# mLSTM heads: from token-major to feature-major by block transposes on VectorE and a DRAM scratch

## The chip, the cores and the metric

The kernel runs on one core of one Trainium2 chip. The metric is the time of one execution in device microseconds (us). In the profile PE is TensorE (PEld its weight loads), DVE is VectorE, ACT is ScalarE, POOL is GpSimd and SP is SyncE, which issues the weight loads from DRAM. Each engine works through its own queue in order. A DMA is issued from an engine's queue, is carried out by the 16 DMA engines, and signals when it has landed.

## What is computed

The reference is a two-layer model on 512 tokens of width 1024: a dilated attention layer, a feed-forward layer, an mLSTM layer and a second feed-forward layer, each with a residual. The change lies in the mLSTM layer. Cut to what matters:

```python
def mlstm_mixer(xn, w_in, conv_w, conv_b, ig_bias, fg_bias, head_gain, w_out):
    proj = xn @ w_in
    ...
    h = mlstm_chunkwise(q, k, vh, ig, lf)          # 8 heads, 512 tokens, 128 values each
    h = h * lax.rsqrt(jnp.mean(h * h, axis=-1, keepdims=True) + RMS_EPS)
    h = h.reshape(B, S, D_MODEL) * head_gain
    return (h * jax.nn.sigmoid(o_pre)) @ w_out
```

For each head a 512 x 128 block of numerators is divided by a denominator for each token, normalized over its 128 values, multiplied by a gate, and all eight heads together go through the output matrix.

## The kernel before

Activations are kept feature-major: a tile has 128 features on the partitions and the 512 tokens along them. Matrix products are made in two parts for precision: each operand is split into a high and a low part, and three matmuls of 128x512 (high-high, high-low, low-high) are added up in PSUM. Weights come in chunks of 512 KB by a DMA on SP into `wraw`; ACT writes the high part (L208) and DVE the low part (L209). In the profile `mqk`, `mv`, `mo` and `mwo` are the products for queries and keys, for values, for the output gate, and with the output matrix; `mwo_k_l` is the low part of a weight chunk of the last of these. `f1j` is the first product of the feed-forward layer that follows.

The mLSTM scan is computed in its quadratic form over 512 tokens, one head after the other, in four steps that are spread over the projections as work to put between them:

- `decay` makes the exponents: a matmul `m0nb` (for head 0) into the PSUM bank of tag `t`, DVE adds the mask (`m0d`), ACT the exponentials (`m0e`).
- `scores` multiplies queries and keys (`m0s`; `ks`, `qs` and `ql` are their split parts, made by `stack`), and DVE multiplies the products into `m0e`.
- `numerators` multiplies by the values (`m0num`, 10 matmuls, which the profile shows as 20 records) into two PSUM banks of tag `o`, of which there are two in all. DVE takes the denominators (`m0rr`), ACT sums the squares (`m0j` into `m0s` of 4 columns), DVE makes an inverse square root by Newton's steps (`m0rq`, small operations on 128x4, each dependent on the last), and four DVE operations scale the numerators into `m0yt` (L1365). This tile is token-major: 128 tokens of a block on the partitions, and four blocks of 128 features next to each other.
- `outputs` turns it: four PE transposes of 128x128 into a bank of tag `t` (`m0yT`, L305), and one ACT copy into `y` (L1374), which is feature-major.

`HEAD_AT` gives for each head the ticks at which the four steps are put into the program; a tick passes with each chunk of a projection. The framework that builds the queues then orders the instructions of each engine by what it expects to be ready, so that small pieces of one step stand between matmuls of a projection, and a change in one place also moves instructions elsewhere.

During `mo` the gate is multiplied in: DVE scales (`og`, L1397), ACT takes a tanh (L1398), DVE multiplies it into `y` (L1399). At the end `y` is split by ACT into `yo_h` (L226) and by DVE into `yo_l` (L227), and `mwo` reads these. `mwo` goes through pairs of 128 output features; each pair takes the heads 0 to 3 and then 4 to 7. Its results are added to the residual `hn` by DVE (L790).

Elsewhere the kernel has the path that the change uses here. In the attention layer `turn` puts values through a DVE transpose of 32x32 blocks (`a3vB`, L673), four DMAs on POOL for each into DRAM (`a3vD`, L675) and one read back (`a3v`, L677); the last layer does the same with the residual (`hB` L1427, `hD` L1430, `ht` L1437).

Of the kernel before, what the change touches and what calls it, by code (L numbers as in the profile page):

```python
# [11 lines left out]
F32 = mybir.dt.float32  # L12
F32R = mybir.dt.float32r
I32 = mybir.dt.int32
AF = mybir.ActivationFunctionType
ALU = mybir.AluOpType
AX = mybir.AxisListType
P = 128

SEQ = 512  # L20
D = 1024
KC = D // P
TB = SEQ // P
# [11 lines left out]
RUN_AT = (2, 3, 5, 10)  # L35
LAST_AT = (2, 4)
STACK_AT = (9, 11, 15, 17)
HEAD_AT = ((9, 10, 12, 14), (10, 11, 13, 15), (12, 13, 15, 17), (13, 14, 16, 18), (15, 16, 18, 19), (16, 17, 19, 21),
           (18, 19, 21, 22), (19, 20, 21, 23))
W_BUFS = 3  # L40
SPLITS = [(0, 0), (0, 1), (1, 0)]

# [28 lines left out]
def tile_hybrid_dilated_attn_mlstm(  # L71
# [4 lines left out]
    nc = tc.nc  # L76
# [3 lines left out]
    def pool(stack, name, **kw):  # L80
        return stack.enter_context(tc.tile_pool(name=name, bufs=1, **kw))
# [4 lines left out]
    ps = pool(ctx, "psum", space=bass.MemoryType.PSUM)  # L86
# [96 lines left out]
    def rsqrt_newton(tp_pool, v, n, name, y=None):  # L183

        if y is None:
            y = tp_pool.tile([P, n], F32, tag="rs_y%d" % n, name=name + "_y", bufs=2)
        a = tp_pool.tile([P, n], F32, tag="rs_a%d" % n, name=name + "_a", bufs=2)
        nc.vector.tensor_single_scalar(a.bitcast(I32), v.bitcast(I32), 1, op=ALU.arith_shift_right)
        nc.vector.tensor_scalar(y.bitcast(I32), a.bitcast(I32), -1, 0x5F3759DF, op0=ALU.mult, op1=ALU.add)
        for _ in range(3):  # L190
            nc.vector.scalar_tensor_tensor(a, y, -0.5, y, op0=ALU.mult, op1=ALU.mult)
            nc.vector.tensor_tensor(a, a, v, op=ALU.mult)
            nc.vector.scalar_tensor_tensor(y, a, 1.5, y, op0=ALU.add, op1=ALU.mult)
        return y
# [8 lines left out]
    def split_chunk(chunk):  # L203

        raw, n, view, name = chunk
        hi = wp.tile([P, 1024], F32R, tag="whi", name=name + "_h", bufs=W_BUFS)
        lo = wp.tile([P, 1024], F32R, tag="wlo", name=name + "_l", bufs=W_BUFS)
        nc.scalar.activation(hi[:, :n], raw[:, :n], AF.Copy)  # L208
        nc.vector.tensor_tensor(lo[:, :n], raw[:, :n], hi[:, :n].bitcast(F32), op=ALU.subtract)  # L209
        return view(hi), view(lo)  # L210
# [4 lines left out]
    def weight_chunk(w2d, ch, c0, n, name):  # L215

        src = w2d[ch * 4 * P:(ch * 4 + n) * P, c0:c0 + 256].rearrange("(k p) n -> p k n", p=P)
        return load_chunk(src, [P, n, 256], name)
# [85 lines left out]
    def transpose_into(dst_ps, i, src, n=P):  # L304
        nc.tensor.transpose(dst_ps[:, i * n:(i + 1) * n], src, ident)  # L305
# [36 lines left out]
    npl = pool(ctx, "norm")  # L342
    h = [hp.tile([P, SEQ], F32, tag="h", name="h%d" % k, bufs=KC + 1) for k in range(KC)]

    with ExitStack() as actx:
# [3 lines left out]
        R = 32  # L349
# [758 lines left out]
    with ExitStack() as fctx:  # L1108
        fp = pool(fctx, "ffn0")
        a, ready = ffn_in(0, fp, pair, rbc, hook,  # L1110
                          lambda ch: split_chunk(weight_chunk(ffn_w_out[0], ch, 0, 4, "fo0_k%d" % ch)))
# [16 lines left out]
    w_in2 = mlstm_w_in[0]  # L1128
    with ExitStack() as mctx:
        mp = pool(mctx, "mlstm")  # L1130
        H = HEADS
        blk = lambda t: t.rearrange("p (b s) -> p b s", b=TB)
        FB = 32 * (TB - 1) + H

        def y_tile(k, name):
            return mp.tile([P, SEQ], F32, tag="my%d" % k, name=name)
# [23 lines left out]

        vaug = mp.tile([P, TB, H, P + 1], F32, name="vaug")
        for tb in range(TB):
# [11 lines left out]

        graw = mp.tile([P, KC, 2 * H], F32, name="graw")
        nc.scalar.dma_start(graw, w_in2[:, 3 * D:3 * D + 2 * H].rearrange("(k p) n -> p k n", p=P))
        bias2 = mp.tile([H, 2], F32, name="gbias")
        nc.scalar.dma_start(bias2[:, 0:1], mlstm_ig_bias.rearrange("o h -> h o"))
        nc.scalar.dma_start(bias2[:, 1:2], mlstm_fg_bias.rearrange("o h -> h o"))

        sel = mp.tile([P, H, P], F32R, name="sel")
        nc.gpsimd.memset(sel.bitcast(F32), 0.0)
# [83 lines left out]
        i = 0  # L1266
# [23 lines left out]
        def stack(p):  # L1290

            for i in range(2):
                own, oth = slice(i * 64, i * 64 + 64), slice(64 - i * 64, 128 - i * 64)
                q, k = qk[p][own], qk[4 + p][own]
                ks = mp.tile([P, SEQ], F32R, tag="ks%d" % i, name="ks%d_%d" % (p, i), bufs=2)
                qs = mp.tile([P, SEQ], F32R, tag="qs%d" % i, name="qs%d_%d" % (p, i), bufs=2)
                nc.scalar.activation(ks[own], k, AF.Copy)  # L1297
                nc.vector.tensor_tensor(ks[oth], k, ks[own].bitcast(F32), op=ALU.subtract)
                nc.scalar.activation(qs[own], q, AF.Copy)
                nc.scalar.activation(qs[oth], q, AF.Copy)  # L1300
                ql = mp.tile([P, SEQ], F32R, tag="ql%d" % i, name="ql%d_%d" % (p, i), bufs=2)
                nc.vector.tensor_tensor(ql[own], q, qs[own].bitcast(F32), op=ALU.subtract)
                nc.gpsimd.tensor_copy(ql[oth], ql[own].bitcast(F32))
                stacks[2 * p + i] = (ks, qs, ql)

        y = [None] * H
        decays, sms, yts = {}, {}, {}

        def decay(hh):
            nm = "m%d" % hh  # L1310
# [25 lines left out]
        def numerators(hh):  # L1336
            nm = "m%d" % hh
            sm = sms[hh]
            num = [ps.tile([P, 512], F32, tag="o", name=nm + "num", bufs=2) for _ in range(2)]
            nv = lambda qb: num[qb // 2][:, (qb % 2) * 256:(qb % 2) * 256 + P + 1]  # L1340
            for qb in range(TB):
                for kb in range(qb + 1):
                    o = (qb - kb) * P
                    nc.tensor.matmul(nv(qb), sm[kb][:, o:o + P], vaug[:, kb, hh, :],
                                     start=(kb == 0), stop=(kb == qb))

            rr = mp.tile([P, TB], F32, tag="rr", name=nm + "rr", bufs=2)
            aa = mp.tile([P, TB], F32, tag="aa", name=nm + "aa", bufs=2)
            s2 = mp.tile([P, TB], F32, tag="s2", name=nm + "s2", bufs=2)
            for t in range(2):  # L1350
                den = num[t].rearrange("p (a b) -> p a b", a=2)[:, :, P]
                nc.vector.tensor_copy(rr[:, 2 * t:2 * t + 2], den)
            nc.vector.scalar_tensor_tensor(aa, rr, -1.0, rr, op0=ALU.mult, op1=ALU.max)
            nc.vector.tensor_tensor(aa, aa, bcol[:, npair:, hh], op=ALU.max)
            nc.vector.reciprocal(rr, aa)
            for qb in range(TB):
                junk = mp.tile([P, P], F32, tag="junk", name=nm + "j", bufs=2)
                nc.scalar.activation(junk, nv(qb)[:, :P], AF.Square, scale=rr[:, qb:qb + 1],
                                     accum_out=s2[:, qb:qb + 1])
            nc.vector.tensor_scalar(s2, s2, 1.0 / P, EPS, op0=ALU.mult, op1=ALU.add)  # L1360
            rq = rsqrt_newton(mp, s2, TB, nm + "rq")
            nc.vector.tensor_tensor(rr, rr, rq, op=ALU.mult)
            yt = mp.tile([P, SEQ], F32, tag="yt", name=nm + "yt", bufs=2)
            for qb in range(TB):
                nc.vector.tensor_scalar(yt[:, qb * P:(qb + 1) * P], nv(qb)[:, :P], rr[:, qb:qb + 1], None,  # L1365
                                        op0=ALU.mult)
            yts[hh] = yt

        def outputs(hh):
            tp = ps.tile([P, 512], F32, tag="t", name="m%dyT" % hh, bufs=1)  # L1370
            for qb in range(TB):
                transpose_into(tp, qb, yts[hh][:, qb * P:(qb + 1) * P])
            y[hh] = y_tile(hh, "y%d" % hh)
            nc.scalar.activation(y[hh], tp, AF.Copy)  # L1374

        def at_tick(t, fn):
            defer(base + t - tick[0], fn)
        at_tick(8, exponents)
        for p, t in enumerate(STACK_AT):
            at_tick(t, lambda p=p: stack(p))  # L1380
        for hh, ts in enumerate(HEAD_AT):
            for t, fn in zip(ts, (decay, scores, numerators, outputs)):
                at_tick(t, lambda hh=hh, fn=fn: fn(hh))
        for pr, cs in ((2, (0, 2)), (3, (1, 3))):
            for c in cs:
# [22 lines left out]
    with ExitStack() as fctx:  # L1408
# [3 lines left out]
        def load(ch, n):  # L1412
            src = wo[ch * 2 * P:(ch + 1) * 2 * P, n * 512:(n + 1) * 512].rearrange("(k p) n -> p k n", p=P)
            return split_weights(src, [P, 2, 512], "fw%d_%d" % (n, ch))
        a, ready = ffn_in(1, fp, pair, rbc, hook, lambda ch: load(ch, 0))
# [4 lines left out]
        R = 32  # L1420
        dp = pool(fctx, "scratch1", space=bass.MemoryType.DRAM)
        ht, turned = [], []
# [26 lines left out]
        outs, ts = [], {}  # L1449
# [6 lines left out]
        for n in range(2):  # L1456
# [27 lines left out]
            for at, tb, cs in tiles:  # L1484
# [4 lines left out]
                t = ts[tb, n][:, cs]  # L1489
# [52 lines left out]
```

## Time and profile before

| | us |
|---|---|
| median of 3 runs | 1428.79 |
| lowest and highest run | 1428.48, 1428.88 |
| the profiled execution | 1428.88 |
| its span on the core | 1427.1 |
| granted clock of TensorE | 0.999 of full speed |

The profile is of one execution. The span runs from the first to the last instruction; the time of the execution has some 1.8 us around it. The page gives the busy time of each engine and a chain of waits, followed back from the last instruction. In rows of a timeline the columns are start, length, engine, line, operation, output and inputs with their shapes, and in brackets the idle time of the engine before it with what ended it. Rows with "x4" merge four instructions; lengths of neighbours overlap, because an instruction starts before the one ahead has drained. The view of DMAs gives the queue, how many, the size of one, and the microseconds from the issue to the landing.

### The profile page before, as it was taken

The numbers are of one execution on the slowest core, as the hardware profiler recorded it, in microseconds if no ns is written. First come the engines' busy times: TensorE is split into PE (matmuls) and PEld (weight loads), VectorE is DVE, ScalarE is ACT, GpSimd is POOL, SyncE is SP. The second block draws the span as 40 slices with busy tenths as digits, with TensorE's granted clock in tenths as the row PEclk, the third lists the DMA queues.
The fourth block names the chain that finished last, engine by engine and source line by source line (L and its number), as shares of the span: only waits on it lengthen the run. The fifth ranks groups of instructions, "written<-read, shape, count | busy, mean of one in ns | idle before, by whom it ended". The sixth has DMA issues, their size and how long they took to land. (4 is left out here: it accounts for less than half of the span.)

```text
span 1427.1 us, 20255 instructions
## 1 busy us (share of the span) xinstructions
PE 1415.9 (99%) x7986; PEld 1241.2 (87%) x7986; DVE 960.4 (67%) x1679; ACT 603.4 (42%) x1009; POOL 84.8 (6%) x137
## 2 busy tenths in 40 slices
PE   9999999999999999999999999999999999999998
PEld 7888888888888888999998888888888899998887
DVE  7857567567567397787782358897758777888233
ACT  5333224224225353444462233696534354445123
POOL 1011011011002000000000010110000000001001
PEclk9999999999999999999999999999999999999999
DMA  6346236235335434323233232321133332346331
GB/s 193 102 115 201 75 104 191 97 108 151 133 104 145 145 101 133 107 72 118 90 96 96 96 98 74 104 60 60 55 113 96 122 118 83 96 118 180 116 106 72
DMA packets 133688, 158.67 MB, mean 111 GB/s; under 512 B 7060, under 2 KB 121044, under 8 KB 133592
## 3 DMA queue, kind: packets, MB, share of 16 engines
q1 hardware_dynamic: 125616, 131.55, 29.6%
q0 software_dynamic: 6320, 24.69, 6.2%
q8 instruction: 63, 1.03, 0.3%
q10 hardware_dynamic: 1656, 1.12, 0.2%
q14 instruction: 33, 0.27, 0.1%
HBM read 143.18 MB, written 14.16 MB: 110 GB/s over the span
## 5 line engine op out<-in xcount | busy, mean ns | idle before, releaser
L1471 PE MATMUL fin<-fw_l,f1hh 128*128 128x512 f32 (+1 forms) x198 | 72.5, 366 | 0.0
L1471 PE MATMUL fin<-fw_h,f1hh 128*128 128x512 f32 (+1 forms) x198 | 72.4, 366 | 0.0
L1471 PE MATMUL fin<-fw_h,f1hl 128*128 128x512 f32 (+1 forms) x198 | 72.4, 365 | 0.0
L209 DVE TENSOR_TENSOR fo_k_l<-fo_k_w,fo_k_h 128x1024 fp32r<-128x1024 f32 (+1 forms) x24 | 27.2, 1135 | 62.0 <-ACT fo_k_h L208 62.0
L239 PE MATMUL fo<-f0hh,fo_k_h 128*128 128x512 f32 x176 | 68.5, 389 | 0.0
L239 PE MATMUL fo<-f0hl,fo_k_h 128*128 128x512 f32 x176 | 68.5, 389 | 0.0
L239 PE MATMUL fo<-f0hh,fo_k_l 128*128 128x512 f32 x176 | 68.5, 389 | 0.0
L209 DVE TENSOR_TENSOR fw_l<-fw_w,fw_h 128x1024 fp32r<-128x1024 f32 x22 | 27.1, 1233 | 59.9 <-ACT fw_h L208 59.9
L208 ACT ACTIVATE fo_k_h<-fo_k_w 128x1024 fp32r<-128x1024 f32 (+1 forms) x24 | 23.7, 989 | 74.7 <-PE fo L239 74.7
L208 ACT ACTIVATE fw_h<-fw_w 128x1024 fp32r<-128x1024 f32 x22 | 23.3, 1060 | 67.6 <-PE fin L1471 67.0
L1471 PEld LDWEIGHTS fin<-fw_l,f1hh 128*128 128x128 f32 x198 | 37.4, 189 | 6.2 <-DVE fw_l L209 0.2
L1471 PEld LDWEIGHTS fin<-fw_h,f1hh 128*128 128x128 f32 x198 | 37.3, 189 | 6.2
L1471 PEld LDWEIGHTS fin<-fw_h,f1hl 128*128 128x128 f32 x198 | 37.3, 188 | 6.0
L239 PEld LDWEIGHTS fo<-f0hh,fo_k_l 128*128 128x128 f32 x176 | 33.0, 188 | 6.9
L239 PEld LDWEIGHTS fo<-f0hl,fo_k_h 128*128 128x128 f32 x176 | 33.0, 188 | 6.9
L239 PEld LDWEIGHTS fo<-f0hh,fo_k_h 128*128 128x128 f32 x176 | 33.0, 188 | 6.7
L239 PE MATMUL f0j<-n_h,f0j_h 128*128 128x512 f32 x96 | 37.5, 390 | 0.0
L239 PE MATMUL f1j<-n_h,f1j_h 128*128 128x512 f32 x96 | 37.5, 390 | 0.0
L239 PE MATMUL f0j<-n_h,f0j_l 128*128 128x512 f32 x96 | 37.4, 389 | 0.0
L239 PE MATMUL f1j<-n_h,f1j_l 128*128 128x512 f32 x96 | 37.4, 389 | 0.0
L239 PE MATMUL f0j<-n_l,f0j_h 128*128 128x512 f32 x96 | 37.3, 389 | 0.0
L239 PE MATMUL f1j<-n_l,f1j_h 128*128 128x512 f32 x96 | 37.3, 389 | 0.0
(2105 smaller groups left out, 4886.0 us busy)
## 6 DMA issues: line engine op xcount, KB each, us to landing
f0j_w<-in_ffn_w_in_dram SPq DMA_DIRECT2D x28, 512.0 KB, 4.9
f1j_w<-in_ffn_w_in_dram SPq DMA_DIRECT2D x28, 512.0 KB, 4.4
fw_w<-in_ffn_w_out_dram SPq DMA_DIRECT2D x22, 512.0 KB, 3.9
fo_k_w<-in_ffn_w_out_dram SPq DMA_DIRECT2D x20, 512.0 KB, 3.5
awo_k_w<-in_attn_w_out_dram SPq DMA_DIRECT2D x8, 512.0 KB, 7.1
mv_k_w<-in_mlstm_w_in_dram SPq DMA_DIRECT2D x8, 512.0 KB, 3.7
mqk_k_w<-in_mlstm_w_in_dram SPq DMA_DIRECT2D x8, 512.0 KB, 3.9
mo_k_w<-in_mlstm_w_in_dram SPq DMA_DIRECT2D x8, 512.0 KB, 3.7
```

The costliest lines, as they stand in the source:

```text
L208: nc.scalar.activation(hi[:, :n], raw[:, :n], AF.Copy)
L209: nc.vector.tensor_tensor(lo[:, :n], raw[:, :n], hi[:, :n].bitcast(F32), op=ALU.subtract)
L239: nc.tensor.matmul(acc, whl[a][:, k, m * P:(m + 1) * P], pairs[b][kk], start=(kk == 0 and (a, b) == SPLITS[0]), stop=(kk == nk - 1 and (a, ...
L1471: nc.tensor.matmul(acc[i][:, cs], a[a_][kk][:, tb * P:(tb + 1) * P], whl[b_][:, k, cs], start=(kk == 0 and (a_, b_) == SPLITS[0]), stop=(k ...
```

## The change

`outputs` is gone, and `HEAD_AT` has three ticks for each head in place of four. Right behind the scaling, `numerators` now transposes `yt` on DVE in blocks of 32x32, one instruction for 128x512. What is left is to bring the blocks to their places. Four DMAs on POOL, one for each quarter of the partitions, write them into a DRAM tile of 128 x 512, in pieces of 32 numbers (128 bytes), 64 KB each; a fifth DMA on POOL reads that tile into `y`, in rows of 2 KB. The fifth waits for the landing of the four. The block-transposed tile takes the tag `sq` of the pool `norm`, with two bufs, which the norms also use; the DRAM tile has three bufs. PE and ACT have no part in it any more. `y_tile` is as before. For each head there are five DMAs more on POOL's queue, which until then held in this stage only the copies of `ql` (L1303).

```diff
-HEAD_AT = ((9, 10, 12, 14), (10, 11, 13, 15), (12, 13, 15, 17), (13, 14, 16, 18), (15, 16, 18, 19), (16, 17, 19, 21),
-           (18, 19, 21, 22), (19, 20, 21, 23))
+HEAD_AT = ((9, 10, 12), (10, 11, 13), (12, 13, 15), (13, 14, 16), (15, 16, 18), (16, 17, 19), (18, 19, 21),
+           (19, 20, 21))
...
         mp = pool(mctx, "mlstm")
+        mdp = pool(mctx, "scratchm", space=bass.MemoryType.DRAM)
+        R = 32
...
-        decays, sms, yts = {}, {}, {}
+        decays, sms = {}, {}
...
             for qb in range(TB):
                 nc.vector.tensor_scalar(yt[:, qb * P:(qb + 1) * P], nv(qb)[:, :P], rr[:, qb:qb + 1], None,
                                         op0=ALU.mult)
-            yts[hh] = yt
-
-        def outputs(hh):
-            tp = ps.tile([P, 512], F32, tag="t", name="m%dyT" % hh, bufs=1)
-            for qb in range(TB):
-                transpose_into(tp, qb, yts[hh][:, qb * P:(qb + 1) * P])
+
+            turned = npl.tile([P, SEQ], F32, tag="sq", name=nm + "yB", bufs=2)
+            nc.vector.transpose(turned.rearrange("p (c i) -> p c i", i=R), yt.rearrange("p (c i) -> p c i", i=R))
+            d = mdp.tile([P, SEQ], F32, tag="yD", name=nm + "yD", bufs=3)
+            for a in range(TB):
+                nc.gpsimd.dma_start(d.rearrange("(f j) (q a i) -> a j q f i", f=4, q=TB, a=4)[a],
+                                    turned[R * a:R * (a + 1)].rearrange("p (q f i) -> p q f i", q=TB, f=4))
             y[hh] = y_tile(hh, "y%d" % hh)
-            nc.scalar.activation(y[hh], tp, AF.Copy)
+            nc.gpsimd.dma_start(y[hh], d)
...
-            for t, fn in zip(ts, (decay, scores, numerators, outputs)):
+            for t, fn in zip(ts, (decay, scores, numerators)):
                 at_tick(t, lambda hh=hh, fn=fn: fn(hh))
```

## The prediction

> **What bounds the kernel now.** I read the page first: the busy shares, the clock row and the chain of waits.
>
> ```profile
> span 1427.1 us, 20255 instructions
> PE 1415.9 (99%) x7986; PEld 1241.2 (87%) x7986; DVE 960.4 (67%) x1679; ACT 603.4 (42%) x1009; POOL 84.8 (6%) x137
> ...
> PEclk9999999999999999999999999999999999999999
> ```
>
> PE is busy 99% of the span at an undisturbed clock. So the kernel is as long as PE's queue, and a change counts only by what it takes out of that queue or by how long it leaves PE waiting. The second view is the busy time by stretches of the mLSTM stage, where the change sits (columns: stretch, PE, PEld, DVE, ACT, POOL busy, clock, DMA share, GB/s).
>
> ```profile
> 940.00:950.00 10.00, 10.00 (x72) 9.09 (x71) 9.94 (x25) 9.91 (x25) 1.12 (x1) 1.00 0.19 54
> 950.00:960.00 10.00, 8.32 (x72) 8.15 (x71) 9.57 (x23) 8.45 (x14) 1.75 (x2) 1.00 0.19 54
> 960.00:970.00 10.00, 10.00 (x60) 8.81 (x59) 5.86 (x23) 7.41 (x24) 0.00 (x0) 1.00 0.19 53
> ...
> 1020.00:1030.00 10.00, 10.00 (x46) 8.26 (x45) 8.15 (x27) 9.34 (x20) 0.00 (x0) 1.00 0.01 2
> 1030.00:1040.00 10.00, 10.00 (x47) 8.04 (x46) 7.47 (x13) 4.10 (x6) 0.11 (x1) 1.00 0.51 154
> ```
>
> Two things are to be seen. DVE is full from 940 to 960, and there PE has its only gap of the stage (8.32 of 10). Afterwards PE is dense again and DVE has room. The third view, the chain of waits in order of time, shows where a delay would start to count (columns: start, length, what):
>
> ```profile
> 971.59 2.23 PE m3num L1344 x20
> ...
> 1017.60 2.23 PE m7num L1344 x20
> ...
> 1027.45 3.17 PE mwo L239 x14
> 1031.66 39.92 PE mwo L239 x176
> 1071.59 5.44 PE f1j L239 x24
> ```
>
> From the numerators of head 7 on the chain is PE work without a break. One dense matmul costs 39.92 / 176 = 0.2268 us.
>
> **What is removed.** Thirty-two PE transposes (4 for each of 8 heads) and eight ACT copies. Four transposes are priced where they stand between known work, in the timeline of PE:
>
> ```profile
> 1030.23 0.39 PE L239 MATMUL mwo<-yo_l,mwo_k_h 128*128 128x512 f32 x1
> ...
> 1031.73 0.39 PE L239 MATMUL mwo<-yo_h,mwo_k_l 128*128 128x512 f32 x1
> ...
> L305 PE MATMUL m7yT<-cst,m7yt x4: 270/273/301, 1030.6 to 1031.4; 128*128 128x128 f32 x4
> ```
>
> Between these two mwo matmuls lie three more and the four transposes. Four steps at 0.2268 are 0.91; the rows are 1.50 apart; so four transposes add 0.59, one 0.148, and all 32 add 4.75 us. ACT is no bound in any stretch but 940 to 960, so its eight copies count as nothing there; they hide behind PE's work, and uncovered they would be 0.6 us each.
>
> **The gap in 950 to 960 does not go.** It looks as though it belonged to a transpose:
>
> ```profile
> 957.55 1.13 DVE L1365 TENSOR_SCALAR m1yt<-m1num,m1rr 128x128 f32<-128x128 f32 x4
> ...
> 958.05 0.30 PE L305 MATMUL m1yT<-cst,m1yt 128*128 128x128 f32 x1 [1.68 <-ACT vaug L1169]
> ...
> 958.54 0.39 PE L1344 MATMUL m2num<-vaug,m2e 128*128 128x129 f32 x2
> ```
>
> The releaser named is ACT, but the first block of m1yt was done at about 957.9 and the transpose follows it: DVE is what was late. Next in the queue stand the numerators of head 2, which need the PSUM banks that m1yt reads, two bufs for two banks of a head. They take over the same wait. DVE gets the block transpose of head 0 into this full stretch (0.7), gets m4d (0.6) ahead of m1yt, and loses two ks subtractions of 0.7 to behind it, so it arrives about as early as before. I cost this place at no gain from the gap.
>
> **What the heads' own chain takes back.** Every head's numerators wait in the same way for the scaling of the head before. At head 2 to 3:
>
> ```profile
> 970.53 1.13 DVE L1365 TENSOR_SCALAR m2yt<-m2num,m2rr 128x128 f32<-128x128 f32 x4
> ...
> 1016.57 1.13 DVE L1365 TENSOR_SCALAR m6yt<-m6num,m6rr 128x128 f32<-128x128 f32 x4
> ...
> 1017.44 2.39 PE L1344 MATMUL m7num<-vaug,m7e 128*128 128x129 f32 x20
> ```
>
> m2yt ends at 971.66, while m3num starts at 971.59 (its first bank was free halfway through m2yt); m6yt is half through at 1017.1, m7num starts at 1017.44. PE comes to the numerators with only 0.3 to 0.5 us to spare, and each interval now loses some 0.6 us of PE work (and some moved matmuls), while DVE's small dependent operations stay. DVE's new transpose stands behind the scaling, where DVE waits for the next numerators anyway, so it costs nothing here; without that cover it would be 0.7 for each head. The stall lies between 0 (DVE, relieved of moved work, keeps ahead) and 3.0 us (20 transposes of 0.148 between m2num and m7num, all given back). I take 1.0, nearer to the lower end, because DVE is only 59% busy in 960 to 970 and its order has moved m4d and m6d out of two of the paths.
>
> **What is added: the tail.** For heads 0 to 5 the way through DRAM has 12 us or more before its result is multiplied. Head 7 has not. I set a clock to 0 at the end of m7num, 1017.44 + 2.39 = 1019.83. In the new order of PE's queue 97 dense matmuls stand between m7num and the first that reads head 7's product: 97 x 0.2268 = 22.0, and the low half is read one matmul later, at 22.2. The durations for DVE and ACT:
>
> ```profile
> 1022.28 0.17 DVE L1360 TENSOR_SCALAR m7s<-m7s 128x4 f32<-128x4 f32 x1 [1.65 <-ACT m7j L1358]
> ...
> 1030.07 1.12 DVE L1365 TENSOR_SCALAR m7yt<-m7num,m7rr 128x128 f32<-128x128 f32 x4
> 1031.11 1.22 DVE L209 TENSOR_TENSOR mwo_k_l<-mwo_k_w,mwo_k_h 128x1024 fp32r<-128x1024 f32 x1
> 1032.39 0.69 DVE L1399 SCALAR_TENSOR_TENSOR y<-og,y 128x512 f32<-128x512 f32 x1
> 1034.14 0.75 DVE L227 SCALAR_TENSOR_TENSOR yo_l<-y,halfgain,yo_h 128x512 fp32r<-128x512 f32 x1
> ...
> 1033.12 0.73 ACT L226 ACTIVATE yo_h<-y,halfgain 128x512 fp32r<-128x512 f32 x1 [0.76 <-DVE y L1399]
> ```
>
> DVE is packed from m7s to m7yt, which ends at 1031.19, 11.4 on the clock. In the new order one mwo_k_l (1.22) moves ahead of it and one yo_l (0.75) behind it: 11.8. That yo_l makes it 12.6. For the block transpose and the DMAs the trace has the same shapes in the attention stage: a 128x512 block transpose, four POOL writes of 64 KB in 128-byte pieces, and a read.
>
> ```profile
> L673 DVE STREAM_TRANSPOSE a3vB<-a3vf x2: 711/712/712, 425.8 to 433.4; 128x512 f32<-128x512 f32 x2
> ...
> 434.45 2.57 POOL L675 DMA_DIRECT2D a3vD<-a3vB  x4 [5.00 <-DVE a3nb L607]
> 439.33 0.77 POOL L677 DMA_DIRECT2D a3v<-a3vD  x1 [2.30 <-DMA a3vD<-a3vB]
> ...
> hD<-hB POOLq DMA_DIRECT2D x8, 256.0 KB, 6.1
> ht<-hD POOLq DMA_DIRECT2D x2, 1024.0 KB, 6.8
> a0v<-a0vD POOLq DMA_DIRECT2D x1, 512.0 KB, 4.2
> a3v<-a3vD POOLq DMA_DIRECT2D x1, 512.0 KB, 4.6
> ```
>
> Transpose 0.7: 13.3. Four issues 2.6: 15.9. The last write lands 2.3 later: 18.2. The read's issue 0.8: 19.0. Its landing, 256 KB, is not in the trace: below it lies the 2.3 of a 64 KB write, above it the 4.6 of a 512 KB read and, for heavy traffic, the 6.8 of 1024 KB. I take 3.6, somewhat under the 512 KB reads, the nearest rows: 22.6. Multiply 0.69, high half 0.73, low half 0.75: 24.7. PE waits 24.7 - 22.2 = 2.5 us. With the read at 2.3 it is 1.2; with a read of 6.8 and a write landing 2.3 later than taken (as long as the longest read row, 4.6) it is 8.0. DVE stands at the multiply from about 15.7 on, and behind it are only the low half of head 7 and the residual additions, which need PE anyway. POOL has nothing but this chain left.
>
> Head 6 needs its product earlier, but its read lands at about 7.6 by the same steps and is multiplied at 10, so it has 2.4 to spare. After head 7, the next bank of mwo waits for a residual addition behind three matmuls (0.68) instead of a full block: about 0.3 more. SP's weight loads keep their order.
>
> [...]
>
> **The sum.** The profiled execution took 1428.88, its span is 1427.1, and the median of the runs is 1428.79. 1428.88 - 4.75 + 1.0 + 2.5 + 0.3 = 1427.93; less 0.09 to the median, 1427.8 us.
>
> **The rivals.** First, *hidden tail*: DVE reaches the block transpose of head 7 some 2 us before 13.3, the read lands by 20, and DVE keeps ahead in all heads. Then PE waits for nothing more and the time is 1428.8 - 4.75 + 0.3 = 1424.3. For it: PE's new order gives head 7 22 us. Against: from 13.3 on even the shortest landings above bring the low half only to 23.4. Chance 0.20.
>
> Second, *late product, slower than before*: the two landings of head 7 run beside the mwo weight loads (DMA share 0.51 in 1030 to 1040) and take what the hD and ht rows took. From a wait of 3.5 us on, that is a chain 1.0 longer than I take, the change loses; at the 8.0 above the time is 1427.8 + 5.5 = 1433.3. Against it: the attention rows were taken under similar traffic. Chance 0.16.
>
> Third, *DVE bound*: the heads give back all 3.0, the first two heads give back their 1.2, and the transpose of head 0 delays the full stretch by 0.7. 1428.8 - 4.75 + 3.0 + 1.2 + 0.7 + 2.8 = 1431.7. For it: DVE at 9.9 and 9.6 of 10 there. Against: 5.9 just after. Chance 0.12.
>
> [...] Chance 0.05. [...]
>
> **How the numbers follow.** My forecast has 0.47. About 0.2% (2.9 us) is what can be told from no change. Faster by more, below 1425.9, is the first rival and the end of my forecast without stalls in the heads and with the shortest read (1428.8 - 4.75 + 1.2 + 0.3 = 1425.6): 0.23. Slower by more, above 1431.7, is the second rival and half of the third: 0.21. Within: 0.56. The range reaches to near the first rival and past the third, 1424.7 to 1432.2; the forecast's own is 1426 to 1430.
>
> **What would show it.** PE without yT rows and 4.7 us less work. A PE wait of 1 to 4 us at the first mwo matmul with head 7's yo_h, put down to ACT or DVE. m2num still waiting about 1.7 for m1yt. Small waits at m3num to m6num. Four yD issues of 0.65 and a write landing of about 2.3. I am wrong if PE has no wait at mwo, if the read lands under 2.5 or over 6 us, or if the waits of the heads add up to more than 3 us.

## The result and the profile after

The changed kernel takes 1431.76 us (median of 19 runs, 1429.69 to 1432.94) where the kernel before takes 1428.92 beside it (19 runs, 1428.20 to 1430.67). The ratio is 1.0019, with a 95% interval of 1.0012 to 1.0025: a loss of 2.8 us, where a gain of about 1 was forecast. The profiled execution of the changed kernel took 1432.5 us, at a mean granted clock of 0.996.

The top of its page:

```profile
span 1430.7 us, 20292 instructions
...
PE 1416.0 (99%) x7954; PEld 1240.0 (87%) x7954; DVE 964.9 (67%) x1687; ACT 599.3 (42%) x1001; POOL 112.6 (8%) x177
```

PE has 32 instructions fewer and is busy for as long as before (1416.0 against 1415.9). Some 4.7 us of work went and the busy time didn't: some of the work that is left must have taken longer. The list of what PE waited for, in the changed kernel (engine, what waits, who was late, us in total, times, longest):

```profile
PE mwo L239 <- ACT yo_h L226: 3.7, 1, 3.7
...
PE m2num L1346 <- DVE m1yt L1367: 1.1, 1, 1.1
...
PE m6num L1346 <- DVE m5yt L1367: 0.2, 1, 0.2
```

The new wait is at the first matmul of the output projection that reads head 7, at the place and from the releaser that the prediction named; it is 3.7 us. The prediction's 2.5 isn't quite the same wait: it counts up to the low half, and up to the high half, to which the profile puts these 3.7, the prediction's clock has 22.6 + 0.69 + 0.73 - 22.0 = 2.0. The heads' own waits are small (two more of 0.2 follow below these rows). The chain of waits of the changed kernel, in order of time, shows how the 3.7 come about:

```profile
927.82 2.23 PE m0num L1346 x20
...
1014.85 2.47 PE m7num L1346 x20
...
1030.74 1.48 POOL m7yD L1374 x2
...
1032.45 5.51 DMA m7yD<-m7yB
...
1038.57 2.93 DMA y<-m7yD
1041.52 0.70 DVE y L1402
1042.25 0.73 ACT yo_h L226
1043.02 32.17 PE mwo L239 x129
1075.19 5.44 PE f1j L239 x24
```

Head 7's numerators start at 1014.85, 2.6 us earlier than before (1017.44): up to there the change gains. The FFN's first matmul starts at 1075.19, 3.6 later than before (1071.59). Behind it nothing differs. The whole loss is made in these 60 us.

The timeline of POOL in the changed kernel has the issues (in brackets its idle time before them):

```profile
1032.45 1.47 POOL L1374 DMA_DIRECT2D m7yD<-m7yB  x2 [0.23 <-issue]
...
1038.57 0.56 POOL L1377 DMA_DIRECT2D y<-m7yD  x1 [4.64 <-DMA m7yD<-m7yB]
```

On the prediction's clock (0 at 1017.32, the end of m7num) the block transpose ends at 13.1, forecast 13.3. The four issues take 0.74 each, 0.09 more than forecast, and end at 1033.92, which is 16.6 for 15.9. Then POOL stands idle for 4.64 us until the writes have landed, where the forecast took 2.30 from the same kind of row; the read's issue starts at 21.25 for 18.2. From there the read takes 2.9, where issue and landing were 0.8 + 3.6 = 4.4 in the forecast (the 2.93 of the chain is counted from the start of the issue, so the forecast's 0.8 stands in its sum twice), and half of the delay is made good: the product is multiplied at 24.2 for 22.6. The view of DMAs of the changed kernel (KB each, median us to landing) shows that the late landing holds for head 7 and not for head 6:

```profile
mwo_k_w<-in_mlstm_w_out_dram SPq DMA_DIRECT2D x5, 512.0 KB, 4.8
m6yD<-m6yB POOLq DMA_DIRECT2D x4, 64.0 KB, 2.4
y<-m6yD POOLq DMA_DIRECT2D x1, 256.0 KB, 2.9
m7yD<-m7yB POOLq DMA_DIRECT2D x4, 64.0 KB, 4.8
y<-m7yD POOLq DMA_DIRECT2D x1, 256.0 KB, 2.9
```

Then there is a second loss, which no part of the prediction has. The timeline of PE in the changed kernel, around the wait:

```profile
1038.96 0.39 PE L239 MATMUL mwo<-yo_h,mwo_k_l 128*128 128x512 f32 x1
1043.02 0.80 PE L239 MATMUL mwo<-yo_h,mwo_k_h 128*128 128x512 f32 x1 [3.67 <-ACT yo_h L226]
1043.81 0.80 PE L239 MATMUL mwo<-yo_l,mwo_k_h 128*128 128x512 f32 x1
1044.40 0.63 PE L239 MATMUL mwo<-yo_h,mwo_k_l 128*128 128x512 f32 x1
1044.83 0.63 PE L239 MATMUL mwo<-yo_h,mwo_k_h 128*128 128x512 f32 x1
...
1048.51 0.39 PE L239 MATMUL mwo<-yo_h,mwo_k_h 128*128 128x512 f32 x1
```

The second matmul, which reads the low half, starts at 1043.81, 0.79 behind the first; that is some 0.4 to 0.6 us more of waiting, since two of the slow matmuls start 0.43 apart and two at full clock 0.227; the profile counts it as busy time. Behind it a matmul of the same shape takes 0.63 instead of 0.39. In the busy time by short stretches (stretch, length, busy time of PE, PEld, DVE, ACT, POOL, granted clock, DMA share, GB/s) the column behind POOL's says why:

```profile
1041.00:1041.50 0.50, 0.00 (x0) 0.00 (x0) 0.00 (x0) 0.00 (x0) 0.00 (x0) 0.98 0.01 0
...
1042.00:1048.00 6.00, 4.98 (x11) 3.57 (x12) 2.94 (x5) 2.82 (x4) 0.11 (x1) 0.50 0.00 0
1048.00:1048.50 0.50, 0.50 (x3) 0.37 (x2) 0.50 (x1) 0.00 (x0) 0.00 (x0) 0.69 0.00 0
```

The granted clock goes from 1.00 to 0.50 while PE waits, and stays there for 5.3 us after PE has work again. From the means in the first and the last row it falls at 1041.48 and comes back at 1048.31, 6.8 us later. The page's own clock row, in tenths over slices of 36 us, shows only nines; one has to ask for the stretch.

### The profile page after: what moved, and what is told of

The parts are those of the page before. It is cut to its first block, busy times and chain, and to the rows that moved or that the text cites. A ratio compares the mean times of both kernels' runs of the same rounds, so it can differ in the third digit from the quotient of the medians.

```text
span 1430.7 us, 20292 instructions
## 1 busy us (share of the span) xinstructions
PE 1416.0 (99%) x7954; PEld 1240.0 (87%) x7954; DVE 964.9 (67%) x1687; ACT 599.3 (42%) x1001; POOL 112.6 (8%) x177
```

## The experiments

Theory: the change gains in heads 0 to 6 and loses only at head 7, in two ways that follow from one another: its product is late because its writes land beside the weight loads of the output projection, and PE, idle for 3.7 us, loses its clock (0.50 in place of 1.00).

### Which head costs it

Head 7 alone goes back to TensorE's transposes:

```
             yts[hh] = yt
+            if not (hh < 7):
+                return
             turned = npl.tile(...)
...
+        def outputs(hh):
+            if hh < 7:
+                return
+            tp = ps.tile([P, 512], F32, tag="t", name="m%dyT" % hh, bufs=1)
+            for qb in range(TB):
+                transpose_into(tp, qb, yts[hh][:, qb * P:(qb + 1) * P])
```

> Head 7 alone is transposed on TensorE again and copied out of PSUM by ACT, as before the change; heads 0 to 6 keep the block transposes and the DRAM scratch. Theory (late product of head 7): the changed kernel loses its time only at the first output-projection matmul that reads head 7. Its wait of 3.7 us goes, the granted clock stays at 1.00 there and the 2.3 us of slow matmuls behind the wait go, the bank wait of 0.3 goes, four transposes (0.6) come back: 1431.8 - 3.7 - 2.3 - 0.3 + 0.6 = 1426.1 us (1425.3 to 1427). Rival A (the heads' chain and the fuller VectorE cost it): 1430 or more, since seven of eight heads still go the new way. Rival B (the wait costs its 3.7, the lower clock nothing): 1428.4.

Measured: 1426.37 us (1425.72 to 1427.46) against 1428.92 before, ratio 0.9983 (0.9974 to 0.9992). The counterpart has the two conditions turned to `hh == 7`, so that only head 7 goes through DRAM:

> The counterpart: only head 7 goes through the block transpose and the DRAM scratch, heads 0 to 6 are transposed on TensorE as before the change. Theory (late product of head 7): before, less four transposes (0.6), plus a wait of about 3.7 at the first matmul that reads head 7, 2.3 of slow matmuls and 0.3 for the bank: 1428.9 - 0.6 + 6.3 = 1434.6 us (1432.5 to 1435.5). Rival A (the cost lies in heads 0 to 6): within 1 us of before, 1428 to 1430. Rival B (the lower clock costs nothing): 1432.3.

Measured: 1435.89 us (1435.64 to 1436.41), ratio 1.0048 (1.0035 to 1.0062). This is 0.4 above the theory's range, with a wait of 4.7 and a landing of 5.3 us (the median of the four writes) in place of 3.7 and 4.8; the direction is clear. Seven heads by the new way gain 2.5 us, the eighth alone loses 7.0. In the chain of the first of these kernels PE is dense from head 7 on:

```profile
1014.10 2.47 PE m7num L1346 x20
...
1029.05 39.65 PE mwo L239 x174
1068.70 5.44 PE f1j L239 x24
```

174 matmuls in 39.65 are 0.228 each. The rival that the heads' chain or VectorE costs the time falls, and so does the one that the lower clock costs nothing: it has 1428.4 for the first kernel and 1432.3 for the second.

### What the idle TensorE costs

Here the changed kernel gets 14 matmuls that nobody reads, so that PE has work during most of the wait. They are called ahead of the first product with head 7, and the profile has them at 1032.4 to 1035.4; the projection's own matmuls move back by as much:

```
...
+    def keep_warm():
+        wps = ps.tile([P, 512], F32, tag="t", name="warm", bufs=1)
+        with tc.issue_after(last_on_pe()):
+            for i in range(14):
+                nc.tensor.matmul(wps, ones_r, ypair[0][0], start=True, stop=True)
+        fence[0] = last_on_pe()
```

> The changed kernel, with 14 matmuls more whose result nobody reads (14 x 0.227 = 3.2 us) put in front of the second block of the output projection, ahead of the first matmul that reads head 7. TensorE then has work for all but some 0.5 us of the wait. Theory (an idle TensorE loses its clock, and that costs a second time): head 7 is ready at the same moment, the granted clock stays at 1.00 from 1040 to 1050, and the matmuls behind the wait take 0.227 apart: 1431.8 - 2.3 = 1429.5 us (1429 to 1430). Rival (the lower clock is only a sign and costs nothing, or comes whatever TensorE does): 1431.8, or up to 1432.5 if the added matmuls stand in the way.

Measured: 1429.85 us (1428.68 to 1431.37), ratio 1.0007 (0.9998 to 1.0015), 1.9 under the changed kernel. Its chain is the cleanest measurement of the clock's price, because head 7 is ready at the same microsecond (the high half starts at 1042.24 here, at 1042.25 above) and the same 129 matmuls follow:

```profile
1042.24 0.73 ACT yo_h L226
1043.02 29.80 PE mwo L243 x129
```

29.80 against 32.17: the lower clock costs 2.4 us in the profiled execution of the changed kernel. Here useless work on PE made the kernel faster (1429.85 against 1431.76). The single runs of the changed kernel say the same: the only one of the 19 whose mean granted clock is 0.999 took 1429.69 us, and the other 18, with 0.996 to 0.998, took 1430.69 to 1432.94.

With 5 matmuls instead of 14 PE stands idle for 2.5 us:

> As the run with 14 unread matmuls, but with 5 (1.1 us), so that TensorE stands idle for about 2.5 us instead of 0.4. It asks how long an idle time costs the clock: in the changed kernel the granted clock fell 2.1 us after TensorE ran out of work, in the run with head 7 alone 3.3 us after. If the clock falls after a fixed idle time of about 2, it falls here too, and the time is that of the changed kernel, 1431 to 1432. [...]

Measured: 1431.93 us, with runs from 1429.26 to 1432.76; ratio 1.0017 (1.0008 to 1.0026). The clock falls in the profiled execution. The wait of this kernel is put to head 7's high half at 2.5 us, and its stretches are:

```profile
1039.00:1042.00 3.00, 0.78 (x4) 0.32 (x2) 0.69 (x1) 0.53 (x1) 0.00 (x0) 1.00 0.23 87
1042.00:1043.00 1.00, 0.76 (x3) 0.48 (x3) 0.75 (x1) 0.19 (x1) 0.00 (x0) 0.91 0.00 0
1043.00:1046.00 3.00, 3.00 (x8) 2.40 (x8) 1.38 (x2) 1.23 (x2) 0.11 (x1) 0.50 0.00 0
1046.00:1047.00 1.00, 1.00 (x5) 0.78 (x5) 1.00 (x2) 1.00 (x3) 0.00 (x0) 0.88 0.00 0
```

PE runs out at 1039.8 and works again from 1042.24. The clock is still full then, falls at 1042.82 and returns at 1046.24: it goes down after the idle time has ended. Counted from the moment PE ran out of work, the fall comes 3.0 us later here and 2.1 later in the changed kernel (1039.35 to 1041.48). So it is no fixed delay, and an idle time of 2.5 us was enough. The low stretch is 3.4 us here and 6.8, twice as long, in the changed kernel. What sets these lengths, and why the runs of this kernel spread over 3.5 us (1429.26 to 1432.76), no run shows.

### Why the writes land late

The changed kernel with a quarter of the output projection's weight traffic (one block of 128 rows loaded in place of four, and used four times over):

```
+        raw, _, _, _ = load_chunk(src[:, :1], [P, 1, 256], name)
...
+            part = raw[:, :256].unsqueeze(1).to_broadcast([P, n // 256, 256])
+            nc.scalar.activation(view(hi), part, AF.Copy)
+            nc.vector.tensor_tensor(view(lo), part, view(hi).bitcast(F32), op=ALU.subtract)
```

> The changed kernel with a quarter of the weight traffic of the output projection: each 512 KB load brings one of its four blocks of 128 rows, and the two halves (high and low) are made from that block four times over, with instructions of the same size. Left out are three quarters of that weight matrix, so the output is another. Theory (head 7's four 64 KB writes land late because 512 KB loads run in the same microseconds): the last write lands 2.3 to 3.0 after its issue instead of 4.6, the read starts some 1.8 earlier, TensorE waits about 1.9 instead of 3.7, too short to lose the clock: 1431.8 - 1.8 - 2.3 = 1427.7 us (1427 to 1429). Rival (the landing is late by itself, for example because POOL issues or writes descriptors more slowly there): the landing stays at 4 or more, time 1431 to 1432.

Measured: 1428.06 us (1427.39 to 1428.55), ratio 0.9991 (0.9983 to 1.0000). Its view of DMAs:

```profile
mwo_k_w<-in_mlstm_w_out_dram SPq DMA_DIRECT2D x8, 128.0 KB, 2.3
...
m7yD<-m7yB POOLq DMA_DIRECT2D x4, 64.0 KB, 2.7
y<-m7yD POOLq DMA_DIRECT2D x1, 256.0 KB, 2.9
```

The four writes land in 2.7 instead of 4.8, PE's wait falls to 1.3, and all its stretches from 1030 to 1052 have the full clock. POOL's idle time before the read is 2.28 there, as the prediction took it. That this kernel comes to within 0.3 us of the prediction's 1427.8 is partly luck: its wait is shorter than the forecast's, because the read is, and the rest of the change gains less than forecast.

The next kernel leaves the loads alone and lets ACT issue head 7's writes and read:

```
-                nc.gpsimd.dma_start(d.rearrange(...)[a],
+                (nc.scalar if hh == 7 else nc.gpsimd).dma_start(d.rearrange(...)[a],
...
-            nc.gpsimd.dma_start(y[hh], d)
+            (nc.scalar if hh == 7 else nc.gpsimd).dma_start(y[hh], d)
```

> The changed kernel with head 7's four writes to DRAM and its read issued by ACT instead of POOL; heads 0 to 6 stay with POOL. ACT is free from the end of its copy of a weight chunk (1031.4 in the trace) to 1042. Theory: what makes head 7 late are the four issues of 0.74 each and the landing beside the weight loads; from ACT the writes are out before the weight loads start at 1032.7, so they land by about 1034 and the read by about 1037 instead of 1041.5; TensorE waits 0 to 1 and keeps its clock: 1425.5 to 1427.5 us. Rival (the loads of the weights hold up any transfer of these microseconds, whoever issues it): the writes land at 1036 or later, the wait is 1.5 to 3 us: 1428 to 1431.

Measured: 1431.19 us (1430.63 to 1432.65), ratio 1.0016 (1.0007 to 1.0024). I had expected a gain; it is a miss. The rival is nearer, with the time 0.2 above its range and a wait of 3.4, above its 1.5 to 3. The chain of this kernel:

```profile
1031.70 0.65 ACTq L1374
...
1032.38 5.79 DMA m7yD<-m7yB
...
1038.35 2.69 DMA y<-m7yD
```

The last issue starts at 1032.38 and takes 0.65, so it ends at 1033.03, 0.9 us before POOL's last (1033.92). The writes have landed at 1032.38 + 5.79 = 1038.17, where POOL's landed at 1032.45 + 5.51 = 1037.96. So an issue 0.9 us sooner brought nothing. But the theory's condition was not met: the two mwo_k_l subtractions, behind whose ends SP issues the weight loads in the changed kernel, run for 2.31 us from 1030.19 here, one ending at about 1031.4 and the other at 1032.5; the last two writes are issued behind the first of these ends (1031.70 and 1032.38), and from 1033 to 1037 225 to 350 GB/s move in each microsecond. The median of the four landings is 4.8 us, as from POOL. That fits the landing beside the loads, whoever issues the writes; how long ACT's writes take without the loads, and whether a still sooner issue would help, no run shows.

### Covering the late product

If PE's running dry is the whole loss, more work ahead of head 7 must cure it, with all eight heads on the new way and their chain as late as ever. The fourth block of the projection gets a bank from the heads' scores, which are done:

```
-        acc = [acc_tile("%s_%d" % (name, m)) for m in range(2)]
+        acc = [acc_tile("%s_%d" % (name, m)) if (name, m) != ("mwo1", 1)
+               else ps.tile([P, 512], F32, tag="s", name="mwo1_1", bufs=2) for m in range(2)]
```

> The changed kernel; only the fourth block of the output projection accumulates in a PSUM bank of another tag (the heads' score bank, free by then), so that 21 of its matmuls (21 x 0.227 = 4.8 us) come ahead of the first that reads head 7. All eight heads keep the block transposes and the DRAM scratch, and the chain of head 7 takes as long as before. Theory (the whole loss is that TensorE runs out of work there): no wait of more than 0.3 us at that place, clock 1.00 throughout, 1431.8 - 3.7 - 2.4 = 1425.7 us (1425 to 1426.5), 3 below the kernel before the change. Rival (the late product costs somewhere else too, for instance at the residual addition and the normalization behind it): 1427.5 or more.

Measured: 1426.16 us (1425.75 to 1426.92), ratio 0.9980 (0.9971 to 0.9989): 5.6 us under the changed kernel and 2.8 under the kernel before. Its chain has no break, its DMA view still has the late landing, and the clock stays:

```profile
1015.02 2.47 PE m7num L1347 x20
...
1025.23 43.87 PE mwo L239 x192
1069.11 5.44 PE f1j L239 x24
```

```profile
m7yD<-m7yB POOLq DMA_DIRECT2D x4, 64.0 KB, 4.9
```

```profile
1040.00:1050.00 10.00, 10.00 (x44) 7.82 (x43) 7.24 (x9) 5.35 (x7) 0.11 (x1) 1.00 0.31 85
```

A control shows that the bank by itself is worth nothing measurable; it is the kernel before with the same two lines:

> A control: the kernel before the change, with nothing but the other PSUM bank for the fourth block of the output projection. TensorE has no wait at head 7 there (the matmuls of the projection stand 0.227 apart throughout). Theory (the bank is worth something only where head 7 is late): 1428.9 us, within 0.5 of the kernel before. Rival (the fourth bank is an improvement by itself, and the run with it says nothing on the block transposes): 1427.5 or less.

Measured: 1428.92 us (1428.29 to 1429.34), ratio 0.9997 (0.9988 to 1.0006).

## Why the prediction was wrong, step by step

**What bounds the kernel, what is removed.** Right. The end moved with PE's queue and nothing else, and the wait came where the new order of that queue put it.

**The gap at m2num, the heads' give-back.** The wait for m1yt stayed, taken over by m2num as said, at 1.1 for 1.7. For the rest, take the stretch from the first matmul of m0num to the first of m7num in PE's timelines: 1017.44 - 927.35 = 90.1 us before and 1014.85 - 927.66 = 87.2 after. Of these 2.9, two output-gate matmuls that moved behind m7num are 0.45 (34 stand there in the chain now, 32 before). So 2.45 was gained, where 25 transposes of 0.148 less the 1.0 for stalls make 2.7. This term was about right. The numerators themselves show part of the stall: 2.47 for heads 6 and 7 in place of 2.23.

**The whole without the tail's wait.** The forecast for it is -4.75 + 1.0 + 0.3 = -3.45; the run with the fourth bank, in which PE waits for nothing at head 7, shows -2.80. So 0.65 of the miss is here; some 0.25 of it is the head stage above, and where the rest lies is open.

**The tail.** This is the step that failed: "the attention rows were taken under similar traffic", with which the forecast set the rival of the late product aside and took 2.3 for the landing. They were not. The 2.3 is from the last four writes of that stage, issued from 434.45 to 437.02. The busy time by stretches of the kernel before, when they landed (the last two columns are DMA share and GB/s):

```profile
434.00:436.00 2.00, 2.00 (x10) 1.65 (x10) 0.66 (x5) 2.00 (x11) 1.54 (x3) 1.00 0.22 33
436.00:438.00 2.00, 2.00 (x11) 1.65 (x10) 0.00 (x0) 2.00 (x11) 1.02 (x2) 1.00 0.65 98
```

And of the changed kernel, when head 7's landed:

```profile
1032.00:1034.00 2.00, 2.00 (x11) 1.65 (x10) 0.69 (x1) 0.00 (x0) 1.69 (x3) 1.00 0.67 137
1034.00:1036.00 2.00, 2.00 (x10) 1.67 (x9) 0.00 (x0) 0.00 (x0) 0.00 (x0) 1.00 0.87 305
```

98 GB/s at most in 2 us against 305. The trace of the kernel before had the warning. Its view of DMAs has the same writes for all four groups of the attention stage, `a0vD` to `a3vD`, and three of them landed later than the group that the forecast used (3.0, 2.8 and 2.7 against 2.4 in the median of eight); two of the four:

```profile
a1vD<-a1vB POOLq DMA_DIRECT2D x8, 64.0 KB, 2.8
a3vD<-a3vB POOLq DMA_DIRECT2D x8, 64.0 KB, 2.4
```

The second four of `a1vD` went out from 207.77 on, with 285 GB/s and a DMA share of 0.99 from 208 to 210, and took 3.6 in the median and 4.1 at the longest. The measured idle time of 4.64 is 2.3 longer than the term of the sum; with the issues 0.7 later and the read 1.5 shorter, the product is 1.6 late. The second rival had the mechanism, the landing of the writes beside the weight loads (4.8 us, and 2.7 with a quarter of the loads), with a chance of 0.16; its other half did not come, the read took 2.9. The loads meet the writes in particular because two mwo_k_l subtractions stand right behind the block transpose on VectorE and free the raw buffers that SP waits for: they end at about 1031.6 and 1032.7, and SP issues there.

```profile
1031.62 1.47 SPq L200 DMA_DIRECT2D mwo_k_w<-in_mlstm_w_out_dram  x2
```

So the same microseconds that make head 7 ready to leave also start the loads.

**The price of a wait.** The second thing that failed: the sum counts a wait of PE at its length. By that rule the late product gives 1.7 more (3.7 instead of 2.0 up to the high half), 1429.5, a kernel hardly slower than before. In the profiled execution the clock added 2.4 to it. The forecast's own rule that the change loses from a wait of 3.5 on was thus too lenient; none of the rivals holds the clock.

Together: the run with the fourth bank lies 5.6 under the changed kernel, and that is the wait with its clock, where 2.5 was taken: 3.1 too little. With the 0.65 above this is the miss of 3.8, from -1.0 to +2.8. The third rival's time (1431.7) was near the result, but for another reason: VectorE and the heads cost little, so that nearness is luck. POOL's issues took 0.09 longer each than in the prediction's row of four: 0.74 with the subtractions beside them, 0.65 in that row with VectorE hardly working (0.66 of the 2 us from 434, nothing in the next 2, in the rows above). Work on VectorE beside them can have cost no more than that.

## What to carry to other kernels

A duration taken from elsewhere in a trace can be wrong under other DMA traffic: 64 KB writes landed in 2.4 us where at most 98 GB/s moved and in 4.8 where up to 305 did. Before using a landing, compare all rows of that transfer and not one, put the GB/s of its microseconds beside those of the place where it will happen, and ask which loads the same instructions set free. The clock of TensorE fell to 0.50 in all four profiled executions with a wait of 2.5 to 4.7 us at this place, and the wait of 1.3 us in the run with light loads left it at 1.00. Where TensorE is the bound, a wait has to be costed with what the clock may add, 2.4 us in the changed kernel. A late product at the end of a pipeline needn't be made early if the bound engine can be given other work: one PSUM bank for the next block turned this change from a loss of 2.8 us into a gain of 2.8, and turning only the last item back to the short way gained nearly as much.

## What the hardware showed that was not expected

The clock of TensorE fell to 0.50 after an idle time of 2.5 us, and not at once but 0.6 us after work had come back; in the run with ACT's queue, with a wait of 3.4, it fell 1.8 us after:

```profile
1039.00:1043.00 4.00, 0.59 (x2) 0.19 (x1) 1.16 (x2) 0.72 (x1) 0.00 (x0) 1.00 0.27 66
...
1044.00:1045.00 1.00, 1.00 (x5) 0.43 (x3) 0.69 (x1) 0.16 (x1) 0.00 (x0) 0.68 0.00 0
...
1047.00:1048.00 1.00, 1.00 (x4) 0.77 (x4) 1.00 (x2) 0.00 (x0) 0.00 (x0) 0.62 0.00 0
```

These are the stretches of that kernel; PE works again from 1042.55, the clock falls at 1044.36 and is back at 1047.76. It stayed low for 3.4 us in two of the kernels and for 6.8 in the changed one, whose idle time was 3.7, and in the one with only head 7 on the new way, whose wait was 4.7 (from 1045.38 to 1052.21). So two kernels whose waits differ by a microsecond can lose about the same time (1431.93 and 1431.76 us, with waits of 2.5 and 3.7). One execution of each was profiled, and what decides when the clock falls stays open.

Issuing the same four writes from another queue, the last of them 0.9 us sooner, brought their landing no further forward (1038.17 against 1037.96).
